# Four output tiles in the first group of products behind a norm, two in the second

## The chip, the cores and the metric

One core of a Trainium2 chip runs the whole program. Its engines are TensorE (PE, with its weight loads as PEld), VectorE (DVE), ScalarE (ACT), GpSimd (POOL) and SyncE (SP), which here issues transfers. Each takes its instructions in one fixed order. The metric is the device time of one launch in microseconds (us), as the median of the runs. The kernel before took 3246.05 us (three runs: 3246.05, 3238.48, 3255.4).

## What is computed

The reference is two blocks of a network, one after the other, on 256 tokens of width 1024 in float32. All norms but one layer norm are root-mean-square norms, and each of the phases below begins with one.

- First block: retention; product-key experts; a spatial gating unit; product-key experts; a final norm. Its norms are scaled and shifted by a vector that a product with a condition gives.
- Second block, with 16 more tokens in front (272 in all): forgetting attention with 16 heads of width 64; a convolutional feed-forward of width 2816 (ffn0); a gated delta rule with 8 heads of width 128; the feed-forward again (ffn1).

What matters here is how a phase starts:

```python
def rmsnorm(x, gain):
    y = x * rsqrt(mean(x * x, axis=-1) + 1e-6)
    return y * gain
# attention:    q, k, v, og, fl = split(rmsnorm(h) @ w_in);  c = cumsum(log_sigmoid(fl + b_forget))
#               softmax(q k / 8 + c_i - c_j) v
# feed-forward: gelu(conv(h @ w_gate)) * conv(h @ w_up) @ w_down
# delta rule:   silu(conv(h @ w_qkv)), beta and g from two narrow products, then a scan over chunks
# gating unit:  u, v = gelu(h @ w_in + b);  (u * spatial(layernorm(v))) @ w_out
```

## The kernel before, in words

Activations lie with the channels on the partitions: x is 8 tiles of 128 channels by 256 or 272 tokens (KC = 8 k tiles). An output tile, called m, is 128 output channels by all tokens and takes 8 k tiles. Float32 precision comes from splitting both sides in a high and a low part, so that mm3 (lines 399 to 404) issues three products for each k tile, high by high (402), low by high (403) and high by low (404): 24 products for an output tile.

The weights are a stream of 128x128 tiles in the order in which output tiles use them, 8 to an output tile. The class Weights loads 16 tiles at a time, a block of 1 MB for two output tiles (the DMA of line 133 on SP's queue, into the pool `stage` of two buffers), and splits them 4 at a time: such a piece is half an output tile's weights, a cast to `whi` on ACT (143) and a subtraction to `wlo` on DVE (145), or on POOL for every third piece within early(). The class remembers only the block loaded last and the last four pieces; a piece of another block has that block loaded anew. Split pieces go to a pool of four buffers (wpart) and in some phases to more (wmore), which the feed-forward has only once the memory of the phase before is free.

Behind a norm the products start before the root mean square is known. As each tile of x comes, feed() writes hi and lo of x times the gain (225, 226 and, in the norm that joins the two blocks, 287 and 288), and squares of x that TensorE sums over the channels (235, 298). early() (409 to 431) takes a first group of output tiles, k tile by k tile and within a k tile all output tiles of the group, on these; tick() (in the first group after every k tile) lets the delayed sums of squares in. After the last sum ACT and DVE make r, the reciprocal root (480, 481, 306). In the last group, after each k tile, finish(k) puts the normalised tile in place of hi and lo (250, 314, 316, 319, split in 378 and 379). Output tiles of early() are multiplied by r (434, early_out) and handed to the phase; the rest of the phase's tiles (linear) read the normalised ones, so they wait for finish.

In attention and in the delta rule one narrow output tile belongs to early()'s last group: `wf`, which gives the forget gates, or beta and g. From the forget gates forget() makes a running sum on DVE (1137 to 1144), writes it to DRAM (1107) and reads it back as `nb`, each head's row on all 128 partitions (1108). The heads' scores add nb (1224, after the product 1215), the exponentials follow, and TensorE transposes them (1241). The heads' work is woven in between the output tiles of linear by a count of VectorE time.

Six PSUM banks rotate among the output tiles, two more serve long sums. The order on each engine is set when the program is built: a scheduler orders instructions by readiness as it models it, and the engines then keep to that.

Of the kernel before, what the change touches and what calls it, by code (L numbers as in the profile page):

```python
# [20 lines left out]
PSUM = bass.MemoryType.PSUM  # L21
# [4 lines left out]
KC = D // P  # L26
T = 256
# [33 lines left out]
def const_packs():  # L61
    """Constants that follow from the shapes alone: {group: {name: [rows, n]}}."""
# [24 lines left out]
def selector_pack():  # L87
    """[8, 4, 128] selectors that hand rows 2 w and 2 w + 1 to a half of the partitions each."""
    s = np.zeros((8, 4, P), np.float32)
    for w in range(4):  # L90
        s[2 * w, w, :64] = 1.0
        s[2 * w + 1, w, 64:] = 1.0
    return s


def decay_pack():
    """Retention decay, [key in tile, head, key tile, query]."""
# [8 lines left out]
class Weights:  # L106
    """Stream of [128, 128] weight tiles: 16 to a load, split in two float32r parts 4 at a time."""
# [47 lines left out]
class Held:  # L155
    """The first n tiles of a stream, in parts that stay."""
# [15 lines left out]
class Squares:  # L172
    """The sum of the squares of KC tiles over the channels, on all partitions: GpSimd adds up all tiles but the last."""
# [5 lines left out]
    def add(self, i, x, scratch):  # L179
        """Returns what has to be emitted once the squares of tile i are there."""  # L180
# [13 lines left out]
class Norm:  # L194
    """hi + lo of y = x * gain, k tile by k tile as x comes, with a column of the shift, and r = 1/rms of x: products
    start on y, W (x * r * gain + shift) = r * (W y) + W shift, and finish() then puts x * r * gain + shift in its place."""
# [61 lines left out]
class FinalNorm(Norm):  # L258
    """The norm that ends the first block, and the one that begins the second, in one: with z = x * g1,
    r1 = 1/rms(x) and r2 = 1/rms(z * r1), y = z * g2 and r = r1 * r2; finish() puts z * r1 in the place of x."""  # L260
# [8 lines left out]
    def start(self):  # L269
        """The tokens that come before x, which only the second norm is for."""  # L270
# [51 lines left out]
class Kernel:  # L322
# [12 lines left out]
    def more_weights(self, ctx, n):  # L335
        """More room for weights ahead of their use, for a phase that has it."""
# [8 lines left out]
    def begin_banks(self, n):  # L345
        """The PSUM banks that rotate in a phase; two more are for sums over many tiles."""
        self.short = itertools.cycle(f"b{i}" for i in range(n))
# [4 lines left out]
    def row_picker(self, rows, i):  # L352
        """Stationary side of a product that hands row i to all partitions."""
# [5 lines left out]
    def after(self, n, f):  # L359
        """Have f emitted n groups of products later, when its operands will have come."""  # L360
# [48 lines left out]
    def early(self, pairs, pool, banks=None):  # L409
        """The first products of a phase, on what Norm has before the rms is known, two m tiles at a time.  # L410
        pairs: of (weights, m, evict)"""
# [30 lines left out]
    def linear(self, name, kt, mt, hi, lo, n, evict, steps=0, first=0, last=None):  # L442
        """out[m*128 + p, t] = sum_k w[k, m*128 + p] h[k, t], tile by tile to evict."""
# [9 lines left out]
    def linear_rows(self, name, nb, hi, lo, evict, steps=0, banks=None, between=None):  # L453
        """out[t, n] with the tokens on partitions, 512 columns at a time."""
# [20 lines left out]
    def inv_root(self, acc, n, scale, pool, tag="rstd"):  # L475
        """1 / sqrt(acc * scale + eps)"""
# [7 lines left out]
    def log_table(self):  # L484
        """Bring in the activation table that holds both Ln and Exp."""
        self.tc.keep_in_program_order(self.nc.scalar.preload_act_table_set("natural_log_exp_and_others"))

# [33 lines left out]
    def acts_tiles(self, k):  # L521
        """The two parts of the moving operand of a phase."""
        return [self.act.tile([P, k, L], F32R, tag=t, name=t) for t in ("hi", "lo")]

    def ada(self, layer, j, pool, tag, bufs, psum=False, slots=None, acc=None):
        """mod[layer, j] [128, 8]: silu(c) @ ada_w + ada_b, a load of weights at a step"""
# [36 lines left out]
    def side(self, *gens):  # L563
        """Work to be woven into the main stream of matrix products."""
        self.fill = itertools.chain(*gens)

    def step(self, ns):
        """Weave in about ns of VectorE time."""
# [42 lines left out]
    def retention(self):  # L611
        nc = self.nc
        with ExitStack() as ctx:
# [77 lines left out]
            def heads():  # L691
                """The heads, each once its columns of v are there."""
# [1033 lines left out]
```

## Time and profile before

| | |
|---|---|
| median of three runs | 3246.05 us |
| profiled execution, first to last instruction | 3247.9 us |
| TensorE busy | 3125.0 us, 96% |
| VectorE busy | 2273.9 us, 70% |
| ScalarE busy | 1851.3 us, 57% |
| mean granted TensorE clock | 0.978 |

The profiled execution has one core, so its span is its time. Its span is 1.85 us above the median. The phases that the change touches begin at about 1146 us (gating unit), 2267 us (attention), 2500 us (ffn0), 2717 us (delta rule) and 3022 us (ffn1). In a list of waits each line names the waiting instruction, what it waited for, the time in total, the number of times and the longest. In a timeline a row is a run of like instructions: start, busy time, engine, line, what it writes and reads, and in brackets the idle time ahead of it with what ended it. A table of stretches gives the stretch, its length, the busy time of each engine with its instructions, the granted TensorE clock (1.00 is 2.4 GHz, 0.50 is 1.2 GHz), the busy share of the DMA engines and GB/s.

### The profile page before, as it was taken

Reading aid. Unit: us, or ns where it says so; the run is one execution under the profiler, and the core shown is the slowest. Engines: PE = TensorE matmul, PEld = TensorE weight load, DVE = VectorE, ACT = ScalarE, POOL = GpSimd, SP = SyncE. Lnnn points to the kernel's source line nnn. Section 1 sums busy time; section 2 is a strip of 40 time slices with the busy share of each in tenths; the row PEclk is TensorE's granted clock in tenths of the full one; section 3 lists DMA queues with packets and bytes.
Section 4 is the critical chain, followed back from the end, with each engine's and each line's share of the span. In section 5 each row is a group of like instructions: output and inputs, shape, how many; then the busy total and the mean of one; then the engine's idle time right before and its main releaser. Section 6 shows DMA issues by size and latency. Waiting matters only on the chain. (4 is left out here: it accounts for less than half of the span.)

```text
span 3247.9 us, 62718 instructions
## 1 busy us (share of the span) xinstructions
PE 3125.0 (96%) x24317; PEld 2985.7 (92%) x24317; DVE 2273.9 (70%) x4670; ACT 1851.3 (57%) x3495; POOL 525.4 (16%) x476
## 2 busy tenths in 40 slices
PE   6999999999999999999999999999999998999998
PEld 5899999999999978999999999999777998898898
DVE  7777867776777688678677767666655975744784
ACT  4566556665455455555566655555546656834663
POOL 1213441110000003334311100000001001133101
PEclk9999999999999999999999999999989999989999
DMA  6755555557777766446555576665322543310453
GB/s 245 245 192 180 204 192 186 181 180 247 265 265 260 274 228 222 149 173 212 195 179 179 182 266 242 232 235 191 130 78 96 191 173 140 118 41 19 152 187 113
DMA packets 119771, 604.08 MB, mean 186 GB/s; under 512 B 14136, under 2 KB 15336, under 8 KB 61488
## 3 DMA queue, kind: packets, MB, share of 16 engines
q1 hardware_dynamic: 98496, 556.84, 48.6%
q10 hardware_dynamic: 19008, 35.72, 3.0%
q0 software_dynamic: 1968, 7.51, 0.7%
q8 instruction: 190, 3.11, 0.4%
q14 instruction: 109, 0.89, 0.1%
HBM read 565.38 MB, written 34.64 MB: 185 GB/s over the span
## 5 line engine op out<-in xcount | busy, mean ns | idle before, releaser
L402 PE MATMUL bank<-hi,whi 128*128 128x256 f32 (+1 forms) x5968 | 1724.0, 289 | 40.4 <-ACT gs L1022 16.4
L404 PE MATMUL bank<-hi,wlo 128*128 128x256 f32 (+1 forms) x5968 | 1701.6, 286 | 18.9 <-DVE wlo L145 18.5
L403 PE MATMUL bank<-lo,whi 128*128 128x256 f32 (+1 forms) x5968 | 1700.7, 285 | 1.2 <-DVE lo L379 1.2
L143 ACT CAST whi<-stage 128x512 fp32r<-128x512 f32 x1780 | 1075.9, 620 | 980.6 <-PE bank L403 713.1
L145 DVE TENSOR_TENSOR wlo<-stage,whi 128x512 fp32r<-128x512 f32 x1566 | 1090.7, 707 | 537.6 <-ACT whi L143 529.3
L402 PEld LDWEIGHTS bank<-hi,whi 128*128 128x128 f32 x5968 | 1142.0, 191 | 58.5 <-ACT gs L1022 18.3
L404 PEld LDWEIGHTS bank<-hi,wlo 128*128 128x128 f32 x5968 | 1138.8, 191 | 29.5 <-DVE wlo L145 26.4
L403 PEld LDWEIGHTS bank<-lo,whi 128*128 128x128 f32 x5968 | 1138.0, 191 | 4.2 <-DVE lo L379 2.2
L145 POOL TENSOR_TENSOR wlo<-stage,whi 128x512 fp32r<-128x512 f32 x214 | 306.5, 1436 | 748.9 <-ACT whi L143 736.8
L402 PE MATMUL bank<-zh,whi 128*128 128x272 f32 (+1 forms) x736 | 212.0, 288 | 1.0 <-ACT zh L378 1.0
L403 PE MATMUL bank<-zl,whi 128*128 128x272 f32 (+1 forms) x736 | 211.4, 287 | 1.0 <-DVE zl L379 0.9
L404 PE MATMUL bank<-zh,wlo 128*128 128x272 f32 (+1 forms) x736 | 211.3, 287 | 0.0
L964 DVE TENSOR_TENSOR oh<-i,rep 128x512 f16<-128x512 f16 x128 | 106.0, 828 | 70.7 <-PE bank L969 70.7
L971 ACT ACTIVATE gates<-bank 128x512 f32<-128x512 f32 x128 | 142.1, 1110 | 18.1 <-PE bank L969 11.4
L969 PE MATMUL bank<-oh 128*128 128x128 f16 x1024 | 142.2, 296 | 0.0
L403 PEld LDWEIGHTS bank<-zl,whi 128*128 128x128 f32 x736 | 140.4, 191 | 1.8 <-DVE zl L379 1.4
L402 PEld LDWEIGHTS bank<-zh,whi 128*128 128x128 f32 x736 | 140.2, 191 | 1.8 <-ACT zh L378 1.2
L185 POOL TENSOR_TENSOR sqa<-sqa,sq 128x272 f32<-128x272 f32 (+1 forms) x36 | 30.0, 833 | 689.5 <-ACT sq L183 689.5
L404 PEld LDWEIGHTS bank<-zh,wlo 128*128 128x128 f32 x736 | 139.9, 190 | 0.2 <-issue 0.2
L1048 DVE TENSOR_TENSOR gs<-gs,gates 128x512 f32<-128x512 f32 x128 | 88.0, 687 | 62.3 <-DMA gs<-spill 60.6
L969 PEld LDWEIGHTS <-oh 128*128 128x128 f16 x1024 | 104.0, 118 | 6.7
L967 DVE TENSOR_TENSOR oh<-oh,gp 128x512 f16<-128x512 f16 x256 | 97.5, 422 | 4.2
(433 smaller groups left out, 3217.7 us busy)
## 6 DMA issues: line engine op xcount, KB each, us to landing
stage<-in_peer_u SPq DMA_DIRECT2D x128, 1024.0 KB, 4.9
stage<-in_peer_v SPq DMA_DIRECT2D x128, 1024.0 KB, 4.9
adaw<-in_ada_w SPq DMA_DIRECT2D x96, 512.0 KB, 5.1
stage<-in_ffn_up SPq DMA_DIRECT2D x44, 1024.0 KB, 4.8
spill<-gs ACTq DMA_DIRECT2D x128, 256.0 KB, 2.0
gs<-spill SPq DMA_DIRECT2D x128, 256.0 KB, 4.9
stage<-in_ffn_down SPq DMA_DIRECT2D x22, 1024.0 KB, 4.8
stage<-in_peer_query SPq DMA_DIRECT2D x16, 1024.0 KB, 4.8
```

What stands on the lines that cost most here:

```text
L143: k.nc.scalar.copy(hi, src)
L145: eng.tensor_tensor(lo, src, hi.bitcast(F32), op=ALU.subtract)
L185: k.nc.gpsimd.tensor_tensor(self.sum, self.sum, sq, op=ALU.add)
L402: mm(acc, wh, xh, start=first, stop=False, skip_group_check=True)
L403: mm(acc, wh, xl, start=False, stop=False, skip_group_check=True)
L404: mm(acc, wl, xh, start=False, stop=last, skip_group_check=True)
L964: nc.vector.tensor_tensor(oh[:, 0], i12[:, 0, None, ts].to_broadcast([P, NK, 4]), rep, op=ALU.is_equal)
L967: nc.vector.tensor_tensor(oh[:, 1 + w], oh[:, 3], gp[:, w, None, ts].to_broadcast([P, NK, 4]), op=ALU.mult)
L969: nc.tensor.matmul(acc[:, u * P:(u + 1) * P], oh[:, 0, :, u], oh[:, 1 + w, :, u], start=w == 0, stop=w == 1, skip_group_check=True)
L971: nc.scalar.activation(gates[:, :, ts].rearrange("p i t -> p t i"), acc.rearrange("p (t i) -> p t i", t=4), AF.Copy, scale=1.0 / GATE_SCALE)
L1048: nc.vector.tensor_tensor(a, a, self.gates[:, i:i + 2], op=ALU.mult)
```

## The change

In the gating unit, attention, both feed-forwards and the delta rule the first group of early() has the output tiles 0 to 3, not 0 and 1. The second has 4 and 5, not 2 and 3; in attention and the delta rule it has wf and tile 4, not wf and tile 2. linear goes on from the tile after that. The code of early() is the same; only its arguments differ. All other lines of the difference are comments and docstrings.

```diff
--- before.py
+++ after.py
@@ sgu @@
-            self.early([[(w, m, uin), (w, m + 1, uin)] for m in (0, 2)], work)
+            self.early([[(w, m, uin) for m in range(4)], [(w, m, uin) for m in (4, 5)]], work)
...
-            self.linear("sgu_u", KC, 24, self.hi, self.lo, T, uin, 600, first=4)
+            self.linear("sgu_u", KC, 24, self.hi, self.lo, T, uin, 600, first=6)
@@ attention @@
-            self.early([[(w, 0, project), (w, 1, project)], [(wf, 0, forget), (w, 2, project)]], work)
-            self.linear("attn_in", KC, 32, self.hi, self.lo, L, project, STEP_A, first=3, last=24)
+            self.early([[(w, m, project) for m in range(4)], [(wf, 0, forget), (w, 4, project)]], work)
+            self.linear("attn_in", KC, 32, self.hi, self.lo, L, project, STEP_A, first=5, last=24)
@@ ffn @@
-            self.early([[(w, m, conv), (w, m + 1, conv)] for m in (0, 2)], work)
-            self.linear(f"ffn_up{layer}", KC, 44, self.hi, self.lo, L, conv, first=4)
+            self.early([[(w, m, conv) for m in range(4)], [(w, m, conv) for m in (4, 5)]], work)
+            self.linear(f"ffn_up{layer}", KC, 44, self.hi, self.lo, L, conv, first=6)
@@ deltanet @@
-            self.early([[(w, 0, conv), (w, 1, conv)], [(wf, 0, coeff), (w, 2, conv)]], work)
-            self.linear("dn_qkv", KC, 24, self.hi, self.lo, L, conv, first=3)
+            self.early([[(w, m, conv) for m in range(4)], [(wf, 0, coeff), (w, 4, conv)]], work)
+            self.linear("dn_qkv", KC, 24, self.hi, self.lo, L, conv, first=5)
```

In the orders below `stage`, `whi` and the like carry the number of the buffer.

SP's loads at the start of attention; `in_attn_in` is the stream of 32 output tiles, `in_attn_fl` that of wf. Before:

```order
L133 DMA stage_28446<-in_attn_in 128x2048
L133 DMA stage_28540<-in_attn_fl 128x1024
L133 DMA stage_28549<-in_attn_in 128x2048
L133 DMA stage_28722<-in_attn_in 128x2048
L133 DMA stage_28818<-in_attn_in 128x2048
```

Now:

```order
L133 DMA stage_28462<-in_attn_in 128x2048
L133 DMA stage_28478<-in_attn_in 128x2048
L133 DMA stage_28532<-in_attn_in 128x2048
L133 DMA stage_28548<-in_attn_in 128x2048
L133 DMA stage_28636<-in_attn_fl 128x1024
L133 DMA stage_28645<-in_attn_in 128x2048
L133 DMA stage_28840<-in_attn_in 128x2048
```

Before, the stream's blocks come once each, with wf behind block 0. Now blocks 0 and 1 come, then blocks 0 and 1 again, then wf and block 2. The other four phases have the two loads more as well.

ACT at the start of ffn0: line 143 casts a piece of weights, 232 squares the last tile of x, 480 and 481 make r, 1319 takes the first finished output tiles. Before:

```order
L232 ACTIVATE sq_30917<-x_81 128x272
L143 CAST whi_30975<-stage_30938 128x512
L143 CAST whi_30982<-stage_30938 128x512
L480 ACTIVATE r_31012<-bank_30871,eps_79 128x272
L143 CAST whi_31035<-stage_31033 128x512
L481 ACTIVATE r_31012<-r_31012 128x272
L143 CAST whi_31042<-stage_31033 128x512
L1319 ACTIVATE cv_31017<-early_31015,taps_30932 128x272
L1319 ACTIVATE cv_31024<-early_31022,taps_30932 128x272
```

Now:

```order
L232 ACTIVATE sq_30939<-x_81 128x272
L143 CAST whi_30980<-stage_30978 128x512
L143 CAST whi_30987<-stage_30978 128x512
L143 CAST whi_31035<-stage_31033 128x512
L143 CAST whi_31042<-stage_31033 128x512
L480 ACTIVATE r_31106<-bank_30893,eps_79 128x272
L481 ACTIVATE r_31106<-r_31106 128x272
L143 CAST whi_31051<-stage_31049 128x512
L143 CAST whi_31058<-stage_31049 128x512
L1319 ACTIVATE cv_31111<-early_31109,taps_30954 128x272
L1319 ACTIVATE cv_31118<-early_31116,taps_30954 128x272
```

Before, all four pieces behind the last square come from blocks that are loaded once (31033 is block 1). Now the first pair is from block 1 (30978), the second from block 0 loaded anew (31033), and the third from block 1 loaded anew (31049), in front of line 1319.

DVE at the end of attention's early(): 379 belongs to finish, 434 is early_out (its first row here is wf), 1137 to 1144 are forget, 1198 scales queries and keys by their norm. Before:

```order
L434 TENSOR_TENSOR early_28658<-bank_28538,r_28511 128x272
L379 TENSOR_TENSOR lo_23725<-modt_28650,hi_23724 128x272
L1137 TENSOR_SCALAR lf_28661<-early_28658,attn_b_forget_2_28422 16x272
L434 TENSOR_TENSOR early_28679<-bank_28539,r_28511 128x272
L145 TENSOR_TENSOR wlo_28741<-stage_28722,whi_28740 128x512
L145 TENSOR_TENSOR wlo_28765<-stage_28722,whi_28764 128x512
L1141 TENSOR_TENSOR lf_28661<-lf_28661,fe_28660 16x272
L145 TENSOR_TENSOR wlo_28781<-stage_28722,whi_28780 128x512
L1142 SCALAR_TENSOR_TENSOR c_28433<-consts_77,lf_28661 16x272
L145 TENSOR_TENSOR wlo_28821<-stage_28818,whi_28820 128x512
L1144 TENSOR_SCALAR fe_28660<-c_28433 16x272
```

Now:

```order
L434 TENSOR_TENSOR early_28760<-bank_28634,r_28585 128x272
L379 TENSOR_TENSOR lo_23739<-modt_28746,hi_23738 128x272
L1137 TENSOR_SCALAR lf_28763<-early_28760,attn_b_forget_2_28436 16x272
L434 TENSOR_TENSOR early_28781<-bank_28635,r_28585 128x272
L145 TENSOR_TENSOR wlo_28787<-stage_28645,whi_28786 128x512
L145 TENSOR_TENSOR wlo_28803<-stage_28645,whi_28802 128x512
L1198 SCALAR_TENSOR_TENSOR qk_28450<-qk_28450,attn_q_norm_2_28438,bank_28818 128x272
L1141 TENSOR_TENSOR lf_28763<-lf_28763,fe_28762 16x272
L1198 SCALAR_TENSOR_TENSOR qk_28450<-qk_28450,attn_q_norm_2_28438,bank_28821 128x272
L1142 SCALAR_TENSOR_TENSOR c_28447<-consts_77,lf_28763 16x272
L1198 SCALAR_TENSOR_TENSOR qk_28450<-qk_28450,attn_k_norm_2_28440,bank_28824 128x272
L1144 TENSOR_SCALAR fe_28762<-c_28447 16x272
```

The rows from wf's 434 to 1144 have the same members but for the pieces of weights (145), two fewer, and three rows of 1198, which have moved in front of 1144. What the rows do not show is that two more early_outs stand ahead of finish on DVE, and that on TensorE wf comes after four output tiles, not two.

## Rows read from the trace of the kernel before

**Rows 1.** The page: span, busy times, one kind of transfer (issue to landing, us)

```profile
span 3247.9 us, 62718 instructions
PE 3125.0 (96%) x24317; PEld 2985.7 (92%) x24317; DVE 2273.9 (70%) x4670; ACT 1851.3 (57%) x3495; POOL 525.4 (16%) x476
...
stage<-in_ffn_up SPq DMA_DIRECT2D x44, 1024.0 KB, 4.8
```

**Rows 2.** Waits of TensorE around the start of ffn0, 2495 to 2530 us

```profile
PE bank L402 <- ACT hi L225: 3.8, 1, 3.8
PE bank L402 <- ACT whi L143: 2.1, 2, 1.5
```

**Rows 3.** Stretches of ffn0's start (columns in the section on the profile)

```profile
2500.00:2505.00 5.00, 4.99 (x20) 4.76 (x21) 5.00 (x12) 3.01 (x7) 1.60 (x2) 0.51 0.00 0
...
2525.00:2530.00 5.00, 5.00 (x30) 5.00 (x30) 3.67 (x9) 1.98 (x5) 0.00 (x0) 0.66 0.23 39
```

**Rows 4.** ACT's timeline in ffn0

```profile
2510.24 1.13 ACT L143 CAST whi<-stage 128x512 fp32r<-128x512 f32 x2
...
2514.58 0.94 ACT L1319 ACTIVATE cv<-early,taps 128x272 f32<-128x272 f32 x2 [1.48 <-DVE early L434]
```

**Rows 5.** SP's timeline in ffn0: the first load after the start

```profile
2512.23 15.88 SPq L133 DMA_DIRECT2D stage<-in_ffn_up  x3
```

**Rows 6.** Line 133 from 2505 to 2530 us, its three loads

```profile
DMA to landing us min/median/max: 5.5/6.0/6.7
```

**Rows 7.** TensorE's timeline in attention: head 0's transposes, and the pace of products

```profile
2314.70 0.28 PE L1241 MATMUL bank<-consts,p 128*16 128x128 f32 x1
...
2317.97 0.29 PE L402 MATMUL bank<-hi,whi 128*128 128x272 f32 x1
...
2318.35 0.29 PE L402 MATMUL bank<-hi,whi 128*128 128x272 f32 x1
```

**Rows 8.** Waits of TensorE in the gating unit, 1146 to 1176 us

```profile
PE bank L466 <- DVE wlo L145: 3.1, 1, 3.1
```

**Rows 9.** A stretch of the gating unit behind that wait

```profile
1170.00:1172.00 2.00, 2.00 (x6) 1.61 (x5) 2.00 (x3) 0.00 (x0) 0.00 (x0) 0.50 0.87 336
```

**Rows 10.** DVE's timeline in attention, from r to the first scores

```profile
2276.86 0.43 DVE L306 TENSOR_TENSOR r<-r 128x256 f32<-128x256 f32 x1 [1.11 <-ACT r L481]
...
2288.52 0.44 DVE L434 TENSOR_TENSOR early<-bank,r 128x272 f32<-128x272 f32 x1
...
2293.22 0.28 DVE L1144 TENSOR_SCALAR fe<-c 16x272 f32<-16x272 f32 x1
...
2311.07 0.78 DVE L1224 SCALAR_TENSOR_TENSOR p<-bank,ccol,nb 128x272 f32<-128x272 f32 x2 [7.18 <-DMA nb<-cd]
```

**Rows 11.** POOL's timeline in attention: forget's two transfers

```profile
2293.79 0.51 POOL L1107 DMA_DIRECT2D cd<-fe  x1 [20.25 <-DVE ccol L1149]
2297.45 0.57 POOL L1108 DMA_DIRECT2D nb<-cd  x1 [3.15 <-DMA cd<-fe]
```

**Rows 12.** Transfers from 2285 to 2320 us: KB each, issue to landing

```profile
stage<-in_attn_in SPq DMA_DIRECT2D x4, 1024.0 KB, 4.9
nb<-cd POOLq DMA_DIRECT2D x1, 2176.0 KB, 13.5
```

**Rows 13.** Stretches of attention: a load by itself, and nb beside loads

```profile
2294.00:2296.00 2.00, 2.00 (x14) 1.65 (x13) 1.44 (x5) 0.37 (x1) 0.30 (x1) 1.00 0.99 418
...
2300.00:2310.00 10.00, 10.00 (x69) 7.71 (x67) 3.44 (x6) 6.24 (x14) 0.00 (x0) 1.00 0.89 347
```

**Rows 14.** Wait of TensorE at the delta rule's start, 2710 to 2756 us

```profile
PE bank L1403 <- ACT sq L1402: 3.3, 2, 2.9
```

**Rows 15.** Stretches of the delta rule behind its early products

```profile
2737.00:2745.00 8.00, 7.10 (x44) 5.64 (x45) 7.38 (x18) 7.85 (x15) 1.09 (x2) 1.00 0.19 49
2745.00:2750.00 5.00, 2.07 (x8) 0.96 (x8) 3.36 (x10) 4.96 (x10) 0.57 (x2) 0.73 0.37 148
```

## The prediction

> **What bounds the kernel now.** I read the head of the page first: TensorE is busy 3125.0 of 3247.9 us [rows 1], so the program is a chain of products, and the change can only fill or open TensorE's waits. It adds and removes no product. Three products on one k tile start 0.38 us apart from the next three (2317.97 to 2318.35) [rows 7], so an output tile of eight k tiles takes 3.0 us at the full clock and two take 6.0 us. Next I read TensorE's waits at the starts of the five phases. In ffn0 it waits 3.8 us for the first tile of x and 2.1 us, in two pieces, for casts that stand behind the finished tiles on ACT [rows 2], and its granted clock is 0.51 behind the first and 0.66 behind the second wait [rows 3]; ffn1 has the same list. In the gating unit it waits once, 3.1 us [rows 8], and the clock is at 0.50 after it [rows 9]. In the delta rule it waits as long for x as in ffn0, and 3.3 us for squares of finished tiles, 2.9 us of that at once [rows 14], and falls to 0.73 in that stretch [rows 15]. In attention the early products run without a pause, and the point that matters lies later: DVE stands idle 7.18 us for the transfer of nb until 2311.07 [rows 10], and TensorE transposes head 0 at 2314.70 [rows 7], 3.6 us behind it, having no other product ready in its order.
>
> **Part 1: ten more loads.** With two output tiles at a time, the k-by-k order asks for pieces of one block. With four it asks for pieces of blocks 0 and 1 in turn, first their halves for k tiles 0 to 3, then those for 4 to 7. The class remembers one block, so both are loaded twice, as SP's order shows: two more loads in each of five phases. A load takes 4.8 us [rows 1], and 5.5 to 6.7 us where two run together [rows 6]. Nothing is paid for the ten megabytes as such, since the DMA engines are mostly free at the phase starts (busy share 0.00 and 0.23 in ffn0 [rows 3]); what is paid is the wait for the second copy of block 1, which can be issued only when the first has been split.
>
> **Part 2: the feed-forwards.** The four extra products per k tile should fill the wait between tiles of x, but ACT's order says they can't: the pieces for tiles 2 and 3 take the place that p1 and p3 had, behind the last square at 2510.24 [rows 4], because their buffers are not free before. So up to 2510.9 nothing changes. From there 72 early products remain as before, 9.0 us. The last 24 need the third pair of casts, from the second copy of block 1. Its load takes the slot at 2512.23 that block 2 had [rows 5], lands 5.5 to 6.7 us later [rows 6], at 2517.7 to 2518.9, and with a cast (0.6 us, from 1.13 us for two [rows 4]) and a subtraction of the same size the piece is there at about 2519.5. TensorE, with 48 products of 6.0 us from 2510.9, gets there at 2516.9: a wait of 2.6 us. What it costs in the end depends on the wait for the finished tiles behind it. Finish begins with the second group, so it moves along, and DVE has two more early_outs and their convolutions ahead of it. If it no longer holds TensorE, 2.1 us of waits and 1.7 us of lost clock (0.34 of 5.00 us) go [rows 2, 3]: the lower end is 2.6 - 3.8 = -1.2 us. If it holds as before, with the longer of the loads, the upper end is +4 us. I take +2 us for each of the two phases, nearer to the stated wait.
>
> **Part 3: the gating unit.** The same reload, but the norm here folds its sums of squares and the early products run without a wait. From the same landing times I estimate a wait of 0 to 3 us. The 3.1 us wait moves along with finish; should it go, with it go about 2 us of half clock [rows 8, 9], so the ends are -5 and +3, and I take +1.
>
> **Part 4: attention.** This is the largest term. The reciprocal root r waits for the last sum of squares, which TensorE's order now puts behind two more output tiles: 48 products, +6.0 us on 2276.86 [rows 10]. From r to wf's early_out DVE works without a pause for 11.66 us (to 2288.52, the first and the last of 31 rows of its timeline [rows 10]); two more early_outs stand in that stretch, 0.35 us each, so wf's early_out goes from 2288.52 to about 2295.2. From there to the end of forget DVE needs 4.7 us now (2293.22 [rows 10]); three scalings in front of it in place of two subtractions of weights leave that much as it is. The transfer out then starts 0.6 us later and nb another 3.7 us later [rows 11], at 2304.1, and with 13.5 us [rows 12] nb lands at 2317.7, 6.7 us later than now. Head 0's transposes keep their place on TensorE, after the same number of output tiles, and finish, later for the same reason, is not slower per tile. So the 6.7 us pass to TensorE in full: 1 us as the reload's wait ahead, the rest as idle time at the transposes. Behind a pause like this the rows give 5.00 us at a clock of 0.51 (after 3.8 us [rows 2, 3]), 2.4 us more. From there on TensorE has no wait in which it could be given back. Sum +9. The lower end is 0, if nb lands as early as now for want of neighbours; the upper end is +14, if the four pieces of weights behind nb's wait on DVE come late too.
>
> The Trainium skill ("DMA: Bandwidth & Descriptors", section "Issuing engines are not separate DMA queues") says that transfers issued by different engines run on the same 16 DMA engines and interleave. The trace agrees: nb, issued on POOL, took 13.5 us beside SP's weight loads [rows 12], at 0.89 busy share and 347 GB/s [rows 13]. Its consequence against my sum is a rival below.
>
> **Part 5: the delta rule.** Here all first pieces are split before x comes, the buffers are free, and four tiles per k tile really are taken together. TensorE is full in that stretch already, so the group itself gives nothing. r comes 7 us later and finish with it. The wait for the squares (2.9 us [rows 14]) comes from table loads and narrow work of wf on ACT between tile 2 and its squares; with wf behind four tiles more full tiles are there to stand beside that. Idle from 2737 to 2750 are 0.9 and 2.9 us, and the clock takes 0.27 of 5.00 us, 1.4 us [rows 15]: 5 us are at stake, and a reload wait of 0.5 to 1 us stands against them. Ends -5 and +1; I take -2.5.
>
> The Trainium skill ("TensorE: Matmul & The Clock Gate", section "Why this matters for your kernels") asks for long dense bursts of products, since a pause of the engine puts it back to the low clock. By that rule twelve products per k tile in place of six would keep the clock up at the phase starts, and the 5.00 us at 0.51 in ffn0 [rows 3], 2.4 us, would go in both feed-forwards. ACT's order, with the pieces for tiles 2 and 3 behind the last square, keeps them out of that stretch, so I count nothing; the first rival would have it.
>
> **Sum.** 2 x 2 + 1 + 9 - 2.5 = +11.5 us on the traced 3247.9, 3259.4. That execution lay 1.85 us above the median of the runs, so 3257.5 by the median.
>
> **Rivals.** A, faster: the longer group covers the waits. At stake are 3.8 us in each feed-forward with the waits for casts [rows 2, 3], 5 in the gating unit, 5 in the delta rule: 17.6 us, and up to 4.8 with the clock at the two starts. Against it: finish, which ends these waits, is not shortened, only moved. For it: more finished-free tiles stand between r and the first tile that needs finish in the feed-forwards. It gives 3224 to 3235, 3229 in the middle.
>
> B, no change: nb's later start lets the weight loads beside it land first. Its 2176 KB at the 418 GB/s of a load by itself [rows 13] take 5.3 us, with the issue some 7 against 13.5, which takes back 6.5 of its 6.7 us and the clock with it. The Trainium skill's rule on shared DMA engines, named above, is what this rests on. Against it: the loads' own splitting on DVE moves along with finish. It gives 11.5 - 9 = +2.5 us, and 3246 to 3250.
>
> C, slower by over 0.5%: the reload decides. In each phase the early group's last products wait for block 1's second copy; behind the gating unit's wait of 3.1 us the clock was at 0.50 [rows 8, 9], and a stretch of 5.00 us like that costs 2.4 us more. If the wait is as long in ffn0, ffn1 and the gating unit, each costs 3.5 + 2.4 = 5.9 in place of 2, 2 and 1, and if attention goes to its upper end and the delta rule gives nothing, the sum is 17.7 + 14 = +32; with half of that beyond my sum, +22. It gives 3264 to 3278. It decides if the reload in ffn0 lands so late, about 2519.4 (2516.9 + 3.1 - 0.6), that TensorE waits as long as in the gating unit.
>
> **How the numbers follow.** A measurement of this kernel can tell about 0.5%, 16 us, from no change; the bounds are 3229.8 and 3262.3. My forecast has 0.50, mostly within (3246 to 3266 by its terms' bounds; 0.42 within, 0.08 slower). A has 0.17 (0.12 faster, 0.05 within), B 0.15, all within, C 0.18, all slower. That makes 0.12, 0.62 and 0.26. The range from 3232 to 3274 leaves out the better half of A and the end of C; the forecast's own is 3246 to 3266.
>
> **What would show it.** In the profile after: ten more loads of 1 MB; wf's early_out 12 us and more behind an r that is 6 us later, nb landing at 2317 to 2318 beyond the shifts before it, and TensorE idle 5 to 6 us at line 1241 with a half clock behind it; in ffn0 a wait of 2 to 3 us of line 402 for a cast of line 143 in the early group; in the delta rule no 2.9 us wait at 1403. The forecast is wrong if nb's transfer takes much less than 13.5 us, if TensorE comes to line 1241 as late as nb does, or if no early product waits for a reload.

## The result, and the profile after

The changed kernel takes 3261.03 us (11 runs, 3249.04 to 3264.27), the kernel before in the same comparison 3238.48 (11 runs, 3234.49 to 3255.4). The medians lie 22.6 us apart; the estimate from all runs gives a ratio of 1.0053, with a 95% interval from 1.0038 to 1.0067: 17 us slower, 12 to 22. The forecast was 11.5 us, and 3257.5 by the median. The traced executions lie closer together, 3258.0 against 3247.9, because the traced one of before was on the slow side of its own kernel.

The page of the changed kernel, answering to [rows 1]: span, busy times, and the feed-forwards' loads (44 before), in the same columns.

```profile
span 3258.0 us, 62737 instructions
...
PE 3123.1 (96%) x24317; PEld 2979.9 (91%) x24317; DVE 2283.4 (70%) x4674; ACT 1849.2 (57%) x3493; POOL 536.3 (16%) x484
...
stage<-in_ffn_up SPq DMA_DIRECT2D x48, 1024.0 KB, 4.8
```

TensorE does the same products in the same busy time; what is added is time in which it waits. To find it I took the length of each phase between two products that stand on either side of it in both orders; it begins in the tail of the phase ahead (at 2471.05 us for ffn0 in the trace of before). One trace is not enough for that. Each kernel below changes only some phases, so its other phases are repeats of before, and the table counts them so where the orders on the engines are those of before. The delta rule's row leaves out two such traces that stand behind changed feed-forwards (310.7 and 310.4 us); they are taken up at the end.

| phase | not changed there, us (traces) | changed | mean difference | forecast |
|---|---|---|---|---|
| gating unit | 250.6 to 254.3 (9) | 250.2, 251.7, 250.6, 246.5 | -2.4 | +1 |
| attention | 210.8 to 224.5 (9) | 220.3, 214.3, 218.4, 215.6 | +2.0 | +9 |
| ffn0 | 240.4 to 241.1 (6) | 245.8, 246.5 | +5.4 | +2 |
| delta rule | 307.1 to 307.2 (3) | 312.5, 312.6, 313.0, 312.5 | +5.5 | -2.5 |
| ffn1 | 216.4 to 217.6 (6) | 221.0, 222.9 | +5.0 | +2 |

The means add up to +15.5 us, which agrees with the timed 17 and, by luck, with the forecast's sum; single terms do not agree. The gating unit and attention differ by less than they scatter. The feed-forwards and the delta rule make the difference.

Waits of TensorE in ffn0 of the changed kernel, 2490 to 2536 us, answering to [rows 2] (total, times, longest).

```profile
PE bank L402 <- ACT whi L143: 4.5, 3, 2.3
PE bank L402 <- ACT hi L225: 3.8, 1, 3.8
...
PE bank L404 <- POOL wlo L145: 0.9, 2, 0.5
PE bank L404 <- DVE wlo L145: 0.4, 1, 0.4
```

The waits for pieces of weights have grown from 2.1 to 4.5 us, and 0.9 us for POOL's subtractions are new. The 3.8 us for the first tile of x is as before: nothing of it was filled. Of the 4.5 us, 1.3 are for the second copy of block 1, and the longest, 2.3 us, is for block 2. Block 2's load, by its place in SP's order the one issued at 2508.53, had landed by then, at 2515.7. Its cast came late because ACT's work on the finished tiles stood in front of it:

```profile
2513.19 1.14 ACT L143 CAST whi<-stage 128x512 fp32r<-128x512 f32 x2 [4.79 <-DMA stage<-in_ffn_up]
...
2517.02 1.28 ACT L1324 ACT_TABLE_LOAD   x1 [1.86 <-DVE cv L1321]
...
2519.78 1.14 ACT L143 CAST whi<-stage 128x512 fp32r<-128x512 f32 x2
```

Waits at the delta rule's start, 2712 to 2760 us, answering to [rows 14].

```profile
PE bank L402 <- ACT hi L225: 4.4, 1, 4.4
PE bank L402 <- ACT whi L143: 1.2, 1, 1.2
PE bank L1403 <- ACT sq L1402: 0.6, 1, 0.6
```

The 2.9 us wait for squares is gone, as forecast; 0.6 us of it is left, and a wait of 1.2 us for a cast is new. But later in this phase, where TensorE hands the norms of queries and keys to all partitions (line 1416, sixteen narrow products), the changed kernel falls behind. Stretches from the first of these products on, of the kernel before and then of the changed one (columns as in [rows 15]; the granted clock is the third number from the right).

```profile
2810.86:2814.86 4.00, 4.00 (x19) 3.24 (x18) 3.13 (x8) 3.96 (x6) 0.00 (x0) 1.00 0.00 0
2814.86:2818.86 4.00, 4.00 (x19) 3.68 (x17) 2.97 (x6) 2.91 (x6) 0.00 (x0) 0.58 0.10 16
```

```profile
2808.85:2812.85 4.00, 4.00 (x14) 2.75 (x15) 1.82 (x4) 3.46 (x4) 0.00 (x0) 0.73 0.39 119
2812.85:2816.85 4.00, 4.00 (x13) 3.02 (x12) 1.56 (x4) 2.82 (x9) 0.00 (x0) 0.50 0.34 143
2816.85:2820.85 4.00, 4.00 (x11) 2.34 (x10) 3.99 (x9) 2.77 (x5) 0.00 (x0) 0.50 0.01 2
2820.85:2824.85 4.00, 4.00 (x21) 4.00 (x20) 0.00 (x0) 0.00 (x0) 0.00 (x0) 0.56 0.75 262
```

Before, the half clock holds for about 4 us, now for about 14. The cause of the difference is taken up with the experiments.

In attention, DVE's and ACT's timelines and the transfers of the changed kernel, answering to [rows 10] and [rows 12].

```profile
2290.09 0.44 DVE L434 TENSOR_TENSOR early<-bank,r 128x272 f32<-128x272 f32 x1
...
2295.05 0.28 DVE L1144 TENSOR_SCALAR fe<-c 16x272 f32<-16x272 f32 x1
...
2311.16 1.29 DVE L145 TENSOR_TENSOR wlo<-stage,whi 128x512 fp32r<-128x512 f32 x2 [6.90 <-ACT whi L143]
2312.37 0.77 DVE L1224 SCALAR_TENSOR_TENSOR p<-bank,ccol,nb 128x272 f32<-128x272 f32 x2
```

```profile
2310.51 1.14 ACT L143 CAST whi<-stage 128x512 fp32r<-128x512 f32 x2 [3.41 <-DMA stage<-in_attn_in]
```

```profile
stage<-in_attn_in SPq DMA_DIRECT2D x3, 1024.0 KB, 8.6
nb<-cd POOLq DMA_DIRECT2D x1, 2176.0 KB, 10.9
```

The phase begins 8.1 us earlier here than in the trace of before, since the phases ahead ran faster; all that follows is measured from its start. wf's early_out is 9.7 us late (6.7 forecast), nb's issue 8.7 us, and with a transfer of 10.9 us, not 13.5, nb lands 6.1 us late. DVE does not wait for it any more. Two subtractions of weights stand in front of line 1224 and wait, through ACT's cast, for a load that ran beside nb and took 9.7 us; the first score starts 3.5 us after nb is there. Head 0's transposes come 9.7 us late. But TensorE does not wait at the transposes. Its waits from the start of the phase to 2320 us are these:

```profile
PE bank L1197 <- DVE early L434: 2.7, 2, 2.4
PE bank L402 <- ACT whi L143: 1.0, 1, 1.0
PE bank L1215 <- DVE p L1224: 1.0, 1, 1.0
PE bank L404 <- POOL wlo L145: 0.9, 2, 0.6
```

The longest, 2.4 us, is at the product that spreads the norms of queries and keys, for an early_out that comes late behind r. The late first score costs it 1.0 us, at line 1215.

### The profile page after: what moved, and what is told of

Same layout as the page of the kernel before. It is cut to its first block, busy times and chain, and to the rows that moved or that the text cites. A ratio compares the mean times of both kernels' runs of the same rounds, so it can differ in the third digit from the quotient of the medians.

```text
span 3258.0 us, 62737 instructions
## 1 busy us (share of the span) xinstructions
PE 3123.1 (96%) x24317; PEld 2979.9 (91%) x24317; DVE 2283.4 (70%) x4674; ACT 1849.2 (57%) x3493; POOL 536.3 (16%) x484
## 5 line engine op out<-in xcount | busy, mean ns | idle before, releaser
L145 POOL TENSOR_TENSOR wlo<-stage,whi 128x512 fp32r<-128x512 f32 x222 | 313.9, 1417 | 809.6 <-ACT whi L143 787.3
```

What stands on the lines that cost most here:

```text
L145: eng.tensor_tensor(lo, src, hi.bitcast(F32), op=ALU.subtract)
```

## The experiments

**One phase at a time.** Each kernel is the one before with the change's lines of one phase:

```diff
 s1_sgu   sgu:       early([[4 tiles], [2 tiles]]), linear first=6
 s2_attn  attention: early([[4 tiles], [wf, tile 4]]), linear first=5
 s3_ffn   ffn:       early([[4 tiles], [2 tiles]]), linear first=6
 s4_dn    deltanet:  early([[4 tiles], [wf, tile 4]]), linear first=5
```

> Only the gating unit has four and two tiles, all else is the kernel before. Theory 1 (each phase keeps the difference that the two traces show, and these add up): the gating unit is 4 us shorter than before, of which 4 us are TensorE's clock and 0.6 us idle time, the other four phases are as before within 1 us, ratio 0.9988. Rival 1 (the clock in a stretch falls by chance from run to run, whatever the order): the gating unit is within 1 us of before, and the other phases' clock loss differs from before by 2 us and more as well. Rival 2 (the reload decides here too): 1 to 3 us longer.

Measured: ratio 1.0014 (0.9998 to 1.0029), the gating unit 251.7 us. Nine traces with the unchanged one lie between 250.6 and 254.3 us, 252.2 in the mean. The 4 us that my two traces showed are within that scatter. Rival 1 holds against the mean; the one trace of before (254.3) is 2.5 us longer.

> Only attention has the new groups. Theory 1: attention is 4 us longer, made of 3.5 us more idle time of TensorE and no more loss by the clock in the sum; head 0's transposes are 9 to 10 us late, and 5 to 6 us of that come back in the second half of the heads, where the half clock is rarer; ratio 1.0012. Rival 1 (clock by chance): the transposes are 9 to 10 us late again, but the part that comes back is another, so that attention is anywhere from 0 to 10 us longer. Rival 2 (the read-back of nb decides): DVE idles at the first score for the transfer, and attention is 7 to 9 us longer.

Measured: ratio 1.0003 (0.9983 to 1.0022). Attention took 214.3 us, 0.8 less than the mean of the nine unchanged traces, so neither Theory 1's 4 us more nor the range of Rival 1 (0 to 10 us longer) was met. The transposes come 67.9 us after the phase's start, 7.9 later than in the trace of before. In the four traces with the changed attention it is 67.9 to 70.4, in the nine with the unchanged one 59.1 to 60.2 six times and 68.2 to 68.4 three times. I split the time up to them, and from them to the end of the heads, in TensorE's idle time, time lost to the half clock and the rest. Ahead of them the changed attention has 1.9 to 3.5 us more idle time than the trace of before, 3.3 to 6.6 us lost to the clock where that one has none, and 1.8 to 2.5 us of products that have moved to the front. Behind them it has 1.4 to 3 us less of products, and no idle time, like the unchanged one. The half clock there took 10.2, 6.8, 10.2, 5.1, 5.1, 6.8, 3.4, 3.4 and 5.1 us in the unchanged nine, 6.6, 1.7, 5.1 and 1.7 in the changed four. That what comes back differs from trace to trace is as Rival 1 had it. Rival 2 does not hold: no wait for nb is left.

> Only the two feed-forwards have the new groups. Theory 1: each is 4 to 5 us longer than before (2.2 to 3.0 us idle time, the rest the clock), 9 us together, ratio 1.0028; in the early group the products wait 1.3 to 2.4 us for a cast. Rival 1 (half of it is clock by chance): 5 us together, with the idle time alone. Rival 2 (the difference comes from the phases before, through what they leave in the buffers): 0 to 3 us.

Measured: ratio 1.0043 (1.0021 to 1.0065); ffn0 246.5 and ffn1 222.9 us, 5.7 and 5.9 longer than the mean of before. Theory 1 holds, with a little more than it said. In this trace attention, whose order on TensorE is unchanged, took 224.5 us, the longest of all: a load issued 0.6 us behind nb landed after 12.3 us, and TensorE waited for what stands behind its cast on ACT. ACT's and TensorE's rows of that place:

```profile
2301.93 1.14 ACT L143 CAST whi<-stage 128x512 fp32r<-128x512 f32 x2 [6.72 <-DMA stage<-in_attn_in]
```

```profile
2303.27 0.48 PE L1188 MATMUL bank<-consts,vt 128*128 128x128 f32 x1 [4.59 <-ACT v L1189]
```

The nine unchanged traces agree on this. In six the load was issued 0.8 to 1.0 us ahead of nb and took 4.7 to 5.0 us, and the transposes came by 60.2 us. In three (s3_ffn, d19, k4_fresh42) it was issued 0.5 to 0.6 us behind nb and took 12.3 us, TensorE waited 4.6 to 6.2 us at line 1188 (1196 in k4_fresh42), and they came at 68. So the order of these two transfers decides some 8 us of attention by itself, without any change. The delta rule, too, was 3.5 us longer here (310.7) with its order unchanged.

> Only the delta rule has the new groups. Theory 1 (the cluster of narrow products of line 1416 comes at another place, TensorE waits 1.25 us for r there, and the half clock holds for some 14 us in place of 4): 5 us longer, ratio 1.0016, with the granted clock at 0.50 for about 14 us around line 1416. Rival 1 (clock by chance): the idle time's 2.4 us alone, with the half clock at 1416 as short as before. Rival 2 (my forecast): 2.5 us shorter.

Measured: ratio 1.0021 (0.9999 to 1.0043), the phase 312.6 us, 5.4 longer. Its first product of line 1416 comes 3.0 us earlier than before, but that is no gain of 3 us: 492 products of mm3 stand ahead of it, and 516 before, so one output tile of 3.0 us has moved behind it. After the same 492 products the phase is 1.3 us shorter than before (1.0 in the changed kernel, 94.90 us against 95.94). Then it waits 1.25 us for r. At the last product of line 1416, with as many products ahead of it in both, it is 5.4 us longer, and the clock in between is at 0.64, 0.50, 0.50 and 0.66 in four stretches of 4 us. Theory 1 holds. Of the forecast's -2.5 us, 1.0 to 1.3 came, and not by less waiting: up to there TensorE is idle 0.7 to 1.3 us more than before and loses 1.5 to 2.6 us less to the half clock.

Together the four changes of one phase make 0.81% by their ratios, the whole change 0.53%. Each of the four is known to about 0.2% only, so this does not show that the phases act on each other.

**Without reloads.**

```diff
-                self.stage = {b: s}
+                self.stage[b] = s
+                while len(self.stage) > 2:
+                    self.stage.pop(next(iter(self.stage)))
```

> The changed kernel, with a class for the weights that remembers the last two blocks and not one, so that no block is loaded twice: as many loads as before. Theory 1 (the reload is what the early group waits for in the feed-forwards, and finish is not slower): the waits of line 402 for casts in ffn0 and ffn1 behind the last square go, 2 to 3 us each, attention loses 1.6 us of waits, the gating unit and the delta rule 0 to 1 us: 6 to 9 us less than the changed kernel, still some 6 to 9 us more than before. Rival 1 (VectorE's work on four finished tiles, or finish, takes the place of the reload): within 2 us of the changed kernel, with a wait as long at the tiles behind the group. Rival 2 (without reload the longer group covers the waits): as fast as before or faster.

Measured: ratio to before 1.005 (1.0028 to 1.0071), ffn0 245.9 and ffn1 221.3 us: as long as with the reloads. Rival 1 holds, Theory 1 does not. Waits of TensorE in ffn0 (this kernel's lines are 2 higher from 135 on):

```profile
PE bank L406 <- DVE wlo L147: 3.6, 1, 3.6
PE bank L404 <- ACT whi L145: 1.4, 1, 1.4
PE bank L404 <- ACT hi L380: 1.1, 2, 0.8
```

From the last square on TensorE now runs through both groups without a wait, and pays some 6 us behind them. DVE's timeline says why:

```profile
2510.07 1.32 DVE L252 SCALAR_TENSOR_TENSOR modt<-x,norm_ffn_pre,r 128x272 f32<-128x272 f32 x3
2516.28 3.07 DVE L147 TENSOR_TENSOR wlo<-stage,whi 128x512 fp32r<-128x512 f32 x2 [4.89 <-ACT whi L145]
...
2522.65 0.43 DVE L381 TENSOR_TENSOR lo<-modt,hi 128x272 fp32r<-128x272 f32 x1
```

r is there and finish's first three multiplications are done by 2511.4 (252), and then DVE stands still for 4.9 us. The low part of the first normalised tile is written at 2522.65 (381): it goes in place of the raw one, which the second group has to read first. What ends the idle time itself is a subtraction of weights, whose cast waited for a load, so these rows alone do not show that finish is the price; the next run does.

**Without finish in the feed-forwards**, on the kernel without reloads.

```diff
-                if pair is pairs[-1]:
+                if pair is pairs[-1] and not getattr(self, "raw", False):
...
+            self.raw = True     # ffn, ahead of early(); False behind it
```

> The changed kernel without reloads (last two blocks remembered) and, in the two feed-forwards, without the step that puts the normalised tiles in place of the raw ones, so that their output is not the reference's. Theory 2 (after the reload is gone, what the products behind the early groups wait for is that step, which can begin only when the second group has read the tiles, 6 us later than before the change): the waits behind the groups, 5.9 us in ffn0 and as much or less in ffn1, go but for the convolutions' share, and each feed-forward is 5 to 8 us shorter than with the reloads gone alone. Rival (VectorE's convolutions of four finished tiles hold the banks): 0 to 2 us shorter, with a wait as long for a bank.

Measured, in one run and its trace: ffn0 238.5 and ffn1 214.3 us, 7.4 and 7.1 shorter than without reloads alone, where a feed-forward in one order scatters by 1.8 us at most. Theory 2 holds: finish is what the products behind the groups wait for, though this run does not tell its late start from its work. Even with none of its work a feed-forward is only 2.2 and 2.7 us shorter than before, so the early products had little more to give.

**A long second group.** Two tiles, then four, with two blocks remembered.

```diff
-            self.early([[(w, m, conv), (w, m + 1, conv)] for m in (0, 2)], work)
+            self.early([[(w, m, conv) for m in (0, 1)], [(w, m, conv) for m in range(2, 6)]], work)
```

> The kernel before, but in the two feed-forwards two output tiles in the first group and four in the second, with the last two blocks of weights remembered. Theory 2 (the second group covers the step that normalises the tiles; it is that group's length that counts): the waits of 2.5 us behind the groups and the half clock after them go, but block 2 is needed 6 us earlier than before, is issued at the same point and makes the second group wait 3 to 5 us at its start: each feed-forward within 2 us of before, ratio 0.9985 to 1.001. Rival (the first group's length counts): nothing but the wait for block 2 is added, each feed-forward 3 to 5 us longer, ratio 1.002 to 1.003.

Measured: ratio 1.0014 (0.9992 to 1.0036), ffn0 243.3 and ffn1 219.8 us, 2.5 and 2.8 longer than before. Waits in ffn0:

```profile
PE bank L406 <- DVE wlo L147: 4.5, 1, 4.5
...
PE bank L406 <- POOL wlo L147: 0.6, 1, 0.6
```

The waits behind the groups for normalised tiles are gone, and within the groups only 0.6 us are lost to a wait for pieces; but the next tile's pieces, whose subtractions stand on DVE behind finish and behind the finished tiles' convolutions, cost 4.5 us. Neither theory had that, and the lengths lie between the two that were expected. The work on DVE is the same wherever it stands.

**Three tiles in the delta rule's second group.**

```diff
-            self.early([[(w, 0, conv), (w, 1, conv)], [(wf, 0, coeff), (w, 2, conv)]], work)
+            self.early([[(w, 0, conv), (w, 1, conv)], [(wf, 0, coeff), (w, 2, conv), (w, 3, conv)]], work)
```

> The kernel before, but in the delta rule the second group has three tiles, wf and 2 and 3, the first two as before; no block is loaded earlier or twice. Theory 2: the waits behind the early groups, 3.8 us from 2737 to 2750 and the half clock after them, shrink by 2 to 5 us up to the first products of line 1416; at the row products of 1416 the order is cut into clusters as in the changed kernel, which gives back 2 to 5 us: the phase within 2 us of before. Rival (the first group's length gives the gain ahead of 1416): no gain ahead of 1416, the phase 0 to 5 us longer.

Measured: ratio 0.999 (0.9969 to 1.0011), the phase 307.9 us, 0.7 longer. The first product of line 1416 comes 2.8 us earlier, with half an output tile fewer ahead of it; after the same 492 products the phase is 1.5 us shorter than before, and at the last product of line 1416 2.6 us. Behind that 3.3 us go again, all of it at the half clock (16.7 us lost there, 13.4 before). The length is as Theory 2 said, the gain does not need four tiles, but it goes behind the row products and not among them.

**The row products a tile later**, on the kernel with the delta rule's new groups.

```diff
-                if m == 18:
+                if m == 19:
```

> The kernel before with the delta rule's new groups, and r for queries and keys asked for one output tile later (at tile 19, not 18), so that six row products of line 1416 stand together a tile later. Theory 3 (the delta rule gains 2 to 3 us up to line 1416 by the new groups and loses some 8 us there, because TensorE comes before r and its scattered narrow products go on at the half clock): the wait for r of 1.25 us goes, the half clock around 1416 is shorter than 14 us, and the phase is 3 to 7 us shorter than with the new groups alone, about as long as before or 2 us less. Rival (the loss has nothing to do with where 1416 stands): 5 us longer than before again.

Measured: ratio 1.0 (0.9975 to 1.0025), the phase 309.5 us, 3.1 shorter than with the new groups alone, 2.3 longer than before. Stretches around line 1416:

```profile
2818.00:2822.00 4.00, 3.94 (x16) 2.73 (x16) 3.59 (x9) 3.96 (x8) 0.00 (x0) 1.00 0.00 0
2822.00:2826.00 4.00, 4.00 (x20) 3.91 (x20) 3.25 (x7) 2.95 (x5) 0.00 (x0) 0.57 0.13 16
2826.00:2830.00 4.00, 4.00 (x34) 4.00 (x33) 2.52 (x5) 2.12 (x7) 0.00 (x0) 1.00 0.63 252
```

The half clock is back to one stretch of 4 us, and the clock stays at 1.00 up to 2842 us, so its length does hang on where these products stand. Among them the half clock costs 6.8 us in all four traces of the new order, 1.7 us here, and 1.7 to 3.4 in five traces of the order of before. The phase gained about the least that was expected, since 3 us of new waits came at the chunks behind (lines 1505 to 1524).

**Normalised tiles of their own.** In the feed-forwards finish writes to two new tiles right behind the first group's products, with four and two tiles and no reloads (k4_fresh42), and with two and two (k5_fresh22).

```diff
-                if pair is pairs[-1]:
+                if pair is pairs[-1] and not fresh:
...
+            if fresh and pair is pairs[0]:
+                raw = y.hi, y.lo
+                y.hi, y.lo = fresh
+                for k in range(KC):
+                    y.finish(k, pool)
+                y.hi, y.lo = raw
```

> The kernel before, with four and two tiles in the feed-forwards, the last two blocks of weights remembered, and the normalised tiles written to tiles of their own (two more of 8 x 272 columns) as soon as r is there, not in place of the raw ones behind the second group's reads. Theory 2 (the price of four and two is that the normalising step begins 6 us later): the step runs beside the rest of the first group, the wait behind the groups goes, and each feed-forward is 4 to 8 us shorter than with the change and the reloads gone, 1 to 3 us shorter than before: ratio 0.998 to 0.9995. Rival (VectorE's convolutions of six tiles then hold the banks, or the 24 last products wait for casts): as long as before or up to 3 us longer.

> The kernel before, with two and two tiles as they were, but in the feed-forwards the normalised tiles go to tiles of their own as soon as r is there. Theory 2: r and the second group's start lie 1.5 us apart in the kernel before, so little can be had: each feed-forward 0 to 3 us shorter than before. If it is as short as with four and two and tiles of their own, then four and two gives nothing even without its price. Rival (in-place writes cost TensorE nothing in the kernel before): within 0.5 us of before.

Measured: 1.002 (1.0003 to 1.0036) and 1.0023 (1.0008 to 1.0037). With four and two a feed-forward takes 242.3 and 218.6 us, 3.6 and 2.8 less than without reloads alone, less than the 4 to 8 expected, and 1.5 and 1.6 more than before, which is what its rival had; with two and two 242.5 and 217.8, 1.7 and 0.8 more than before, where neither the theory (0 to 3 us shorter) nor the rival (within 0.5 us) was met. So with tiles of their own four and two is no better than two and two. In ffn0 of the former one wait of any size is left behind the first tile of x and the squares:

```profile
PE bank L406 <- DVE wlo L147: 3.0, 1, 3.0
```

Beginning finish early gives back half of the 7 us. The wait that is left is for a subtraction that stands on DVE behind the convolutions of finished tiles (lines 1329 and 1335 here, from 2526.60 to 2530.58). That these make up all of the other half is not shown. No kernel that computes the reference was faster than before.

## Why the prediction came out

The sign and the sum were right, the terms were not: attention came 7 us and the gating unit 3 under their terms, the delta rule 8 and the feed-forwards 3 each over theirs, and but for 4 us these cancelled. That the sum fits is luck.

- **Attention, +9 forecast, about +2 measured.** The chain up to nb came nearly as forecast: r 5.0 us late (6.0), wf's early_out 9.7 (6.7), nb's landing 6.1 (6.7). The step that failed is the next, that the 6.7 us pass to TensorE in full, most of it as idle time at the transposes. TensorE waits 0.5 us at most at line 1241, before and after. It is busy for 10.00 of 10.00 us while nb is on its way [rows 13], so it had other products ready. The late first score cost it 1.0 us. The transposes' 9.7 us are made of other things: 3.5 us more idle time (most of it at lines 1197, 402 and 1215), 3.7 us at the half clock, 2.5 us of products that moved ahead of them. That this is near 9 is luck, and the unchanged order has the transposes at 68 us, too, in three of nine traces. The prediction's own sign of being wrong, TensorE coming to line 1241 as late as nb does, was there. Nor does the delay last: in the mean of all traces the changed order is 7.2 us later at the transposes and 5.2 us quicker behind them, by the products that have moved ahead and by a half clock of 1.7 to 6.6 us in place of 3.4 to 10.2. With four traces against nine, the clock's part may be chance.
- **Feed-forwards, +2 forecast, +5 measured.** The wait for block 1's second copy came where it was forecast (1.3 us, against 2.6), but without the reload nothing was gained. The term was sized by the wrong wait: "finish begins with the second group, so it moves along" was there, but not its price, that DVE idles 5 us with r at hand and then has finish and four convolutions at once. ACT has its share of it: the 2.3 us wait behind is for a cast of block 2 that stands there behind the finished tiles.
- **Delta rule, -2.5 forecast, +5.5 measured.** The wait for squares went, but others came, and by the same work only 1.0 to 1.3 us were gained ahead of line 1416. The step failed behind that: TensorE's changed arrival at the row products was not followed. Between the 492nd product of mm3 and the last row product 6.7 us went, 1.25 us as a wait for r and 5.1 us at the half clock.
- **Gating unit, +1 forecast.** Not resolved; the phase scatters by 4 us.
- **Rivals.** A, that the longer group covers the waits, is ruled out for the feed-forwards: the waits for casts that it wanted gone grew from 2.1 to 4.5 us in ffn0. C's mechanism, the reload, is ruled out there by the kernel without it. B was half true: nb's transfer did become shorter beside fewer loads (10.1 to 10.9 us, against 11.9 to 13.7), and the loads beside it paid.

Open is what sets the half clock off. In s3_ffn and g1_ffn24, which change only the feed-forwards, TensorE, DVE and ACT go through the delta rule in the order of before, and yet it took 310.7 and 310.4 us and not 307.1: 4.3 us more are lost at the half clock, and TensorE is idle 1.2 to 1.5 us less. So 3 us of this phase can come without any change in it, and its +5.5 need not add to the feed-forwards'. In k4_fresh42 and k5_fresh22 (309.6 and 313.1 us) the orders in the delta rule differ from before; I did not take them apart.

## What to carry to other kernels

Where a later step overwrites what early work reads, more early work delays that step: count when the reader is done, not only when the input is there. A second load may make an engine wait and still not be the price; take it away by itself before calling it one. A chain that ends in a late input costs the last engine only what it stands idle for it, so look at that engine's own waits. Compare two orders after the same work, not at a line that has moved. And follow a shift to the next place where the granted clock falls, and repeat a phase's length over several traces before reading 5 us into it.

## What the runs showed that I had not expected

- The length of attention, in one and the same order of instructions on TensorE, ran from 210.8 to 224.5 us over nine traces, by two things: whether a weight load is issued just behind nb, and how long the granted clock stays at 0.50 behind head 0's transposes (3.4 to 10.2 us lost). Four stretches of before, then of the changed kernel:

```profile
2360.00:2380.00 20.00, 20.00 (x111) 13.97 (x109) 12.39 (x39) 8.68 (x28) 0.00 (x0) 0.88 0.29 101
2380.00:2400.00 20.00, 20.00 (x129) 15.88 (x128) 10.36 (x33) 11.07 (x31) 0.00 (x0) 0.95 0.17 59
2400.00:2420.00 20.00, 20.00 (x110) 14.41 (x109) 11.95 (x38) 8.81 (x27) 0.00 (x0) 0.90 0.14 54
2420.00:2440.00 20.00, 20.00 (x116) 15.27 (x115) 8.55 (x28) 11.15 (x24) 0.00 (x0) 0.84 0.16 53
```

```profile
2360.00:2380.00 20.00, 20.00 (x125) 14.63 (x123) 12.90 (x40) 9.13 (x28) 0.00 (x0) 1.00 0.26 93
2380.00:2400.00 20.00, 20.00 (x135) 15.63 (x135) 10.80 (x34) 11.88 (x34) 0.00 (x0) 1.00 0.29 106
2400.00:2420.00 20.00, 20.00 (x120) 13.86 (x120) 12.58 (x38) 8.97 (x29) 0.00 (x0) 1.00 0.16 54
2420.00:2440.00 20.00, 20.00 (x139) 16.32 (x137) 9.82 (x34) 14.89 (x33) 0.00 (x0) 1.00 0.15 53
```

  TensorE is busy throughout in all eight, and the clock still falls in four of them: a busy engine is no sign of the full clock.
- Two of DVE's subtractions of weights took 3.07 us at 2516.28 in the kernel without reloads, where one takes 0.68 us in the rows behind (2523.00), while POOL did two of the same kind (1.29 and 1.43 us, 2515.82 to 2518.80); each of DVE's two ends 0.5 to 0.6 us after one of POOL's. The Trainium skill ("SBUF — State Buffer", section "SBUF: two separate sides") says that a pair of ports is shared, and that an instruction of either engine that needs it, on VectorE one with two operands from SBUF, holds it to its end; these rows agree.
